# Moving the weight tiles of a float32 decoder kernel to another remainder modulo 256 bytes

## The chip, the cores and the metric

The kernel runs on one NeuronCore of a Trainium2 chip. The metric is the device time of one execution in microseconds. Runs of this kernel lay between 2705.7 and 2709.78 us, with a median of 2706.16 us over three runs.

## What is computed

The reference is a two-layer decoder trunk on a sequence of 1,024 tokens with a width of 1,024, in float32. Layer 0 mixes with a short gated convolution, layer 1 with differential attention (8 heads, two maps of 64 dimensions each) over one shared K and V. Each layer also has a causal convolution FFN (width 2,816, gate and up) and a gated embedding from a per-layer input `p`. Every sub-layer is wrapped in RMSNorm. Cut to what matters here:

```python
def short_conv_mixer(h, w_in, w_conv, w_out):
    gb, gc, u = jnp.split(h @ w_in, 3, axis=-1)
    return (gb * causal_dwconv(gc * u, w_conv)) @ w_out

def conv_ffn(h, w_up, w_conv, w_down):
    gate, up = jnp.split(causal_dwconv(h @ w_up, w_conv), 2, axis=-1)
    return (jax.nn.silu(gate) * up) @ w_down

def per_layer_embed(x, p_i, g_pre, w_gate, w_proj, g_post):
    gate = jax.nn.sigmoid(rms_norm(x, g_pre) @ w_gate)
    return rms_norm(gate * (p_i @ w_proj), g_post)
...
for i in range(DEPTH):
    h = rms_norm(x, g_pre_mix[i])
    mix = short_conv_mixer(...) if i < N_A_LAYERS else diff_attention(...)
    x = x + rms_norm(mix, g_post_mix[i])
    x = x + rms_norm(conv_ffn(rms_norm(x, g_pre_ffn[i]), ...), g_post_ffn[i])
    x = x + per_layer_embed(x, p[i], ...)
```

## The kernel before

**Products.** Activations are held transposed: 128 features on the partitions, 512 tokens (one half of the sequence) along a partition. A float32 product is made from three matmuls on operands of type float32r: each operand is split into a high part (a cast) and a low part (the rest), and high x high, low x high and high x low are added up in PSUM. `mm3` (L323 to L329) does this for one output block of 128 features over 8 input blocks: 24 matmuls. The weight is the stationary operand, a slice of 128 columns of a tile `wh` (high) or `wl` (low); the activation is the moving operand, 512 columns of a pair of tiles, most of them from the pool `hy` (40 tiles) or from an "s" tile of the scope that is open.

**Weights.** `wload` (L175) loads a weight block of 512 KB into a tile `wr`; `wsplit` (L189) or `wcut` (L214) makes `wh` on ScalarE and `wl` on VectorE (L206 to L217). Each of `wr`, `wh`, `wl` has three buffers of 4,096 bytes a partition in the pool `wpool`. A loader works two weight blocks ahead, and the splits one ahead of their use (`emit_all`, L289).

**FFN.** The up projection has three kinds of steps. `std_step` (L781, matmul L796) computes one block for the first half of the tokens, in two parts of 256 columns, 24 matmuls each. `pair_step` (L831) computes a gate block and an up block together by a scheme with seven products instead of eight, each of `product` (L813, matmuls L818 to L820) with 12 matmuls; with `both` set it has 512 columns, without it 256. Its last product uses `A22`, whose split is kept in tiles `w5h` and `w5l` of the scope "up" (L226); the other six use `wh` and `wl` tiles (`pair_split`, L220). The first 8 blocks of layer 0 and the first 7 of layer 1 (`NS`) are done by two `std_step` and later one 256-column `pair_step`, the other 14 and 15 by a 512-column `pair_step`. The down projection (`down_step`, L922, matmuls L935 to L937) reads the hidden activations back from DRAM, splits each into a `c2` tile, and runs 512-column matmuls into four PSUM tiles.

**Attention.** `v_part` (L1136, matmul L1151) has the operands the other way round: the activation `hy` is stationary, and 256 columns of `wh` or `wl` move. `kq_part` uses `mm3` with PSUM tiles `pd`. Scores (L1258), transposes (L1284, L1324) and the product with V (L1299) are interleaved with them. Transposes of the norms are at L367 and L379; those and the others read `ident`, the identity matrix.

**Placement.** Tiles are placed one after another within a partition. Outer pools come first: constants (`cst`, `ident`, `halo`, `gsub`, `neg_lam`), `wpool`, `work` (`acc`, `sq`, small ones, `hn`, `rb`), `hypool`. Behind them lies the scope that is open: "sc" for the convolution layer (tiles `rk`, `c`, `u`, then 24 "s" tiles), "up", "pq" or "att". Tiles that nothing uses (`pad0`, `pad1`, `pad`) take place only. The first constant starts 16,512 bytes into the partition.

```python
nc.tensor.matmul(out, whi[:, c], hi, start=(i == 0), stop=False)
nc.tensor.matmul(out, wlo[:, c], hi, start=False, stop=False)
last_mm[0] = nc.tensor.matmul(out, whi[:, c], lo, start=False, stop=(i == n - 1)).ins
```

Of the kernel before, what the change touches and what calls it, by code (L numbers as in the profile page):

```python
# [9 lines left out]
F32 = mybir.dt.float32  # L10
# [6 lines left out]
S = 1024  # L17
HT = 512
UW = 528
ND = 8  # L20
NF = 22
NH = 8
# [35 lines left out]
def program(tc, a):  # L58
    nc = tc.nc
    ctx = ExitStack()  # L60
    with ctx:
        _program(tc, nc, a, ctx)


def _program(tc, nc, a, ctx):
    P = 128
    ep = ctx.enter_context
    cpool = ep(tc.tile_pool(name="cpool", bufs=1))
    wpool = ep(tc.tile_pool(name="wpool", bufs=3))
    work = ep(tc.tile_pool(name="work", bufs=2))  # L70
# [7 lines left out]
    def nm(s):  # L78
        uid[0] += 1
        return f"{s}_{uid[0]}"  # L80
# [17 lines left out]
    def wk(tag, shape=(P, HT), dt=F32, bufs=2):  # L98
        return work.tile(list(shape), dt, tag=tag, name=nm(tag), bufs=bufs)
# [24 lines left out]
    def own(al, t):  # L124
        owner[id(t)] = (al, t)
        return t
# [20 lines left out]
    cst = cpool.tile([P, C_ALL], F32, tag="cst", name="cst")  # L147
    nc.sync.dma_start(out=cst, in_=a["cvec"])

    cpool.tile([P, 8], F32, tag="pad0", name="pad0")  # L150
    work.tile([P, 8], F32, tag="pad", name="pad", bufs=1)
    ident = cpool.tile([P, P], F32, tag="ident", name="ident")
    make_identity(nc, ident)
    cpool.tile([P, 8], F32, tag="pad1", name="pad1")
    halo = cpool.tile([P, 52, 2], F32, tag="halo", name="halo")
    gsub = cpool.tile([P, 1], F32, tag="gsub", name="gsub")
    nc.vector.tensor_scalar(gsub, cst[:, C_SUB:C_SUB + 1], 1.0 - LAM0, None, ALU.mult)
# [6 lines left out]
    oscr = dpool.tile([2, NH, 2, P, HT], F32, tag="oscr", name="oscr")  # L164
    xscr = dpool.tile([2, ND, P, HT], F32, tag="xscr", name="xscr")
    pscr = dpool.tile([2, ND, P, HT], F32, tag="pscr", name="pscr")
    grep = dpool.tile([NH, P, GLEN], F32, tag="grep", name="grep")
# [101 lines left out]
    cur = []  # L269
# [3 lines left out]
    def free_h(key):  # L273
        slots_of[key].free(2 * ND)

# [134 lines left out]
    def make_h(xs, rb, gname, key, alloc, drop=False):  # L410
        hs = []
        al = alloc if isinstance(alloc, Slots) else alloc()
        for k in range(ND):
            while not al.room(2):
# [17 lines left out]
    def prologue():  # L432

        first = [s_ for s_ in steps if s_["w"] is not None][:2]
        for k in range(ND):
            if k in (PR0, PR1):
# [5 lines left out]
    def gen_first(half):  # L442
        xs = first_x if half == 0 else []
        acc = wk("acc", bufs=3)
        for k in range(len(xs), ND):
            x = own(hy, hy())
# [210 lines left out]
        ys.append(y)  # L657

    def su():
        return cur[0].tile([P, UW], F32, tag="u", name=nm("u"), bufs=3)[:, 0:HT + 2]  # L660

    def sc_():
        if "up" in scopes:
# [3 lines left out]
    def u2():  # L667
        return scopes["up"][1].tile([P, 2, UW], F32, tag="u2", name=nm("u2"), bufs=2)[:, :, 0:HT + 2]

# [40 lines left out]
    def sc_mix(half):  # L710
# [15 lines left out]
        def u_step(f):  # L726
            def fn(w):
                p_ = ps()
                mm3(p_, w[0], w[1], have["mix0", half], k128)
                v = su()  # L730
                nc.vector.tensor_tensor(v[:, 2:], hold["gc"], p_, ALU.mult)
                c = conv(None, v, f, half, C_SC + 3 * f, v[:, 2:])
                if half == 0:
                    nc.vector.tensor_tensor(c, c, have["r", ("mix0", 0)][0], ALU.mult)
                hold["c"] = c
            return fn
# [786 lines left out]
```

## Time and profile before

| what | value |
|---|---|
| median of three runs | 2706.16 us |
| the profiled execution | 2703.73 us |
| its span, from the first to the last instruction | 2701.9 us |
| mean granted TensorE clock | 0.98 |
| TensorE matmul busy | 2581.3 us, 96% |
| TensorE weight load busy | 2137.5 us, 79% |
| VectorE busy | 1866.8 us, 69% |
| ScalarE busy | 1296.4 us, 48% |
| GpSimd busy | 158.1 us, 6% |

A matmul's duration in the profile runs from its start to a modelled end and overlaps with the next one; the time that a row of matmuls takes is read from the starts. Weight loads (PEld) run beside the matmul ahead of them. "hy,wh" in a row means that the instruction reads a moving tile of `hy` and a weight tile `wh`; buffer numbers are left out.

### The profile page before, as it was taken

Reading aid. Unit: us, or ns where it says so; the run is one execution under the profiler, and the core shown is the slowest. Engines: PE = TensorE matmul, PEld = TensorE weight load, DVE = VectorE, ACT = ScalarE, POOL = GpSimd, SP = SyncE. Lnnn points to the kernel's source line nnn. Section 1 sums busy time; section 2 is a strip of 40 time slices with the busy share of each in tenths; the row PEclk is TensorE's granted clock in tenths of the full one; section 3 lists DMA queues with packets and bytes.
Section 4 is the critical chain, followed back from the end, with each engine's and each line's share of the span. In section 5 each row is a group of like instructions: output and inputs, shape, how many; then the busy total and the mean of one; then the engine's idle time right before and its main releaser. Section 6 shows DMA issues by size and latency. Waiting matters only on the chain.

```text
span 2701.9 us, 36095 instructions
## 1 busy us (share of the span) xinstructions
PE 2581.3 (96%) x13438; PEld 2137.5 (79%) x13438; DVE 1866.8 (69%) x3201; ACT 1296.4 (48%) x2216; POOL 158.1 (6%) x328
## 2 busy tenths in 40 slices
PE   8999999899998999997999999899899999899995
PEld 7878889688887878786887878788788888787874
DVE  7546459877797466688666665558977779547667
ACT  5233245444455445556555545446544445445542
POOL 0000003000011000000000000100200001000001
PEclk9999999899999999998999999899999999999998
DMA  5225224222236554333111111266222223656342
GB/s 177 99 91 195 94 90 130 86 86 78 83 109 215 187 205 153 122 121 117 47 48 63 56 48 56 97 217 218 95 86 72 86 78 117 232 188 217 109 171 78
DMA packets 125407, 325.30 MB, mean 120 GB/s; under 512 B 14008, under 2 KB 16352, under 8 KB 125232
## 3 DMA queue, kind: packets, MB, share of 16 engines
q1 hardware_dynamic: 125232, 323.01, 35.0%
q8 instruction: 105, 1.72, 0.3%
q14 instruction: 70, 0.57, 0.1%
HBM read 271.54 MB, written 56.14 MB: 121 GB/s over the span
## 4 chain that ended last, share of the span: by engine, by line
PE 85%; DVE 9%; ACT 2%; DMA 2%; issue 2%; DVEq 0%; SPq 0%; ACTq 0%
PE ps L327 8%; PE ps L328 8%; PE ps L329 8%; PE ps L819 7%; PE ps L820 7%; PE ps L818 7%; PE ps L937 6%; PE ps L936 6%; PE ps L935 6%; PE ps L796 4%; PE pd L1151 4%; PE qk L1258 3%; PE st L1299 2%; PE pd L327 2%; PE pd L328 2%; PE pd L329 2%
## 5 line engine op out<-in xcount | busy, mean ns | idle before, releaser
L211 DVE TENSOR_TENSOR wl<-wr,wh 128x1024 fp32r<-128x1024 f32 x238 | 290.9, 1223 | 231.5 <-ACT wh L210 179.4
L210 ACT CAST wh<-wr 128x1024 fp32r<-128x1024 f32 x238 | 249.9, 1051 | 349.9 <-PE ps L937 148.4
L819 PE MATMUL ps<-hy,wl 128*128 128x512 f32 (+1 forms) x924 | 329.8, 359 | 16.8 <-DVE wl L217 16.8
L818 PE MATMUL ps<-hy,wh 128*128 128x512 f32 (+1 forms) x924 | 316.5, 359 | 13.6 <-ACT wh L216 13.6
L935 PE MATMUL ps<-c,wh 128*128 128x512 f32 x704 | 279.6, 397 | 8.8 <-ACT c L314 8.8
L936 PE MATMUL ps<-c,wl 128*128 128x512 f32 x704 | 279.9, 398 | 0.0
L216 ACT CAST wh<-wr 128x1024 fp32r<-128x1024 f32 x132 | 137.8, 1047 | 209.5 <-PE ps L820 154.2
L937 PE MATMUL ps<-c,wh 128*128 128x512 f32 x704 | 231.2, 397 | 2.0 <-DVE c L315 2.0
L327 PE MATMUL ps<-hy,wh 128*128 128x512 f32 x552 | 218.3, 397 | 8.3 <-ACT hy L399 8.3
L820 PE MATMUL ps<-hy,wh 128*128 128x512 f32 (+1 forms) x616 | 219.2, 357 | 0.0
L328 PE MATMUL ps<-hy,wl 128*128 128x512 f32 x552 | 218.4, 396 | 0.0
L329 PE MATMUL ps<-hy,wh 128*128 128x512 f32 x552 | 217.8, 396 | 0.0
L819 PEld LDWEIGHTS ps<-hy,wl 128*128 128x128 f32 x924 | 174.8, 189 | 48.8 <-DVE wl L217 20.9
L818 PEld LDWEIGHTS ps<-hy,wh 128*128 128x128 f32 x924 | 171.8, 190 | 44.4 <-ACT wh L216 16.6
L217 DVE TENSOR_TENSOR wl<-wr,wh 128x1024 fp32r<-128x1024 f32 x132 | 160.8, 1221 | 17.1 <-ACT wh L216 16.9
L935 PEld LDWEIGHTS ps<-c,wh 128*128 128x128 f32 x704 | 132.8, 189 | 41.1 <-ACT c L314 9.3
L937 PEld LDWEIGHTS ps<-c,wh 128*128 128x128 f32 x704 | 132.7, 189 | 35.9 <-DVE c L315 3.8
L936 PEld LDWEIGHTS ps<-c,wl 128*128 128x128 f32 x704 | 132.8, 189 | 32.5
L314 ACT CAST c<-s 128x512 fp32r<-128x512 f32 x175 | 108.1, 619 | 104.4 <-PE ps L937 93.6
L340 DVE TENSOR_TENSOR acc<-acc,sq 128x512 f32<-128x512 f32 x165 | 112.8, 687 | 61.3 <-ACT sq L339 58.9
L820 PE MATMUL ps<-s,wh 128*128 128x512 f32 (+1 forms) x440 | 154.6, 356 | 0.0
L315 DVE TENSOR_TENSOR c<-s,c 128x512 fp32r<-128x512 f32 x175 | 120.2, 688 | 47.8 <-ACT c L314 47.8
(237 smaller groups left out, 5894.8 us busy)
## 6 DMA issues: line engine op xcount, KB each, us to landing
wr<-w_ffn_up SPq DMA_DIRECT2D x118, 512.0 KB, 3.5
wr<-w_ffn_down SPq DMA_DIRECT2D x88, 512.0 KB, 3.5
s<-hscr SPq DMA_DIRECT2D x175, 256.0 KB, 3.5
wr<-w_sc_in SPq DMA_DIRECT2D x48, 512.0 KB, 3.5
hscr<-c SPq DMA_DIRECT2D x88, 256.0 KB, 2.5
wr<-w_ple_gate SPq DMA_DIRECT2D x32, 512.0 KB, 3.5
xscr<-hy SPq DMA_DIRECT2D x40, 256.0 KB, 4.5
hy<-xscr SPq DMA_DIRECT2D x40, 256.0 KB, 5.6
```

Of the source, the lines that this page charges most:

```text
L210: nc.scalar.copy(out=hi[:, :n], in_=raw[:, :n])
L211: nc.vector.tensor_tensor(lo[:, :n], raw[:, :n], hi[:, :n].bitcast(F32), ALU.subtract)
L217: nc.vector.tensor_tensor(lo, src, hi.bitcast(F32), ALU.subtract)
L327: nc.tensor.matmul(out, whi[:, c], hi, start=(i == 0), stop=False)
L328: nc.tensor.matmul(out, wlo[:, c], hi, start=False, stop=False)
L329: last_mm[0] = nc.tensor.matmul(out, whi[:, c], lo, start=False, stop=(i == n - 1)).ins
L818: nc.tensor.matmul(o, hi[:, c], bh, skip_group_check=True, start=start and j == 0, stop=False)
L819: nc.tensor.matmul(o, lo[:, c], bh, skip_group_check=True, start=False, stop=False)
L820: last_mm[0] = nc.tensor.matmul(o, hi[:, c], bl, skip_group_check=True, start=False, stop=stop and j == 3).ins
L935: nc.tensor.matmul(o, hi[:, c], j[:, 0, :], start=(k == 0), stop=False)
L936: nc.tensor.matmul(o, lo[:, c], j[:, 0, :], start=False, stop=False)
L937: last_mm[0] = nc.tensor.matmul(o, hi[:, c], j[:, 1, :], start=False, stop=(k == NF - 1)).ins
```

## The change

Two unused tiles of 32 bytes among the constants are removed, the unused tile in the work pool grows from 32 to 96 bytes, and the tile `u` of the first layer from 2,112 to 2,304 bytes, of which the same part is used. Nothing else differs.

```diff
+US = 576
...
-    cpool.tile([P, 8], F32, tag="pad0", name="pad0")
-    work.tile([P, 8], F32, tag="pad", name="pad", bufs=1)
+    work.tile([P, 24], F32, tag="pad", name="pad", bufs=1)
     ident = cpool.tile([P, P], F32, tag="ident", name="ident")
     make_identity(nc, ident)
-    cpool.tile([P, 8], F32, tag="pad1", name="pad1")
     halo = cpool.tile([P, 52, 2], F32, tag="halo", name="halo")
...
     def su():
-        return cur[0].tile([P, UW], F32, tag="u", name=nm("u"), bufs=3)[:, 0:HT + 2]
+        return cur[0].tile([P, US], F32, tag="u", name=nm("u"), bufs=3)[:, 0:HT + 2]
```

## Rows read from the trace of the kernel before

**Rows 1.** The page: the span, and TensorE's busy time with its share.

```profile
span 2701.9 us, 36095 instructions
...
PE 2581.3 (96%) x13438; PEld 2137.5 (79%) x13438; DVE 1866.8 (69%) x3201; ACT 1296.4 (48%) x2216; POOL 158.1 (6%) x328
```

**Rows 2.** The page: the chain that ended last, shares of the span by engine.

```profile
PE 85%; DVE 9%; ACT 2%; DMA 2%; issue 2%; DVEq 0%; SPq 0%; ACTq 0%
```

**Rows 3.** Busy time by stage: us, each engine's busy us, granted clock, DMA share, GB/s.

```profile
20.00:368.00 348.00, 348.00 (x1506) 277.87 (x1505) 191.03 (x285) 117.58 (x163) 6.00 (x24) 1.00 0.35 116
...
400.00:450.00 50.00, 50.00 (x440) 50.00 (x439) 44.55 (x77) 27.63 (x44) 13.36 (x18) 1.00 0.53 171
477.00:769.00 292.00, 281.87 (x1242) 229.02 (x1243) 226.76 (x254) 133.26 (x170) 22.98 (x59) 0.98 0.24 83
769.00:870.00 101.00, 89.89 (x657) 82.83 (x657) 87.89 (x129) 56.51 (x91) 14.86 (x15) 0.98 0.54 185
870.00:1086.00 216.00, 214.99 (x929) 172.23 (x928) 130.69 (x187) 103.50 (x154) 0.00 (x0) 1.00 0.53 180
1216.00:1745.00 529.00, 504.81 (x3125) 413.05 (x3123) 338.32 (x967) 283.64 (x719) 31.43 (x75) 0.97 0.19 65
```

**Rows 4.** Groups of matmuls by shape: 512 columns, weight wh (busy us, mean ns).

```profile
L935 PE MATMUL ps<-c,wh 128*128 128x512 f32 x704 | 279.6, 397 | 8.8 <-ACT c L314 8.8
...
L818 PE MATMUL ps<-hy,wh 128*128 128x512 f32 x610 | 235.7, 400 | 13.6 <-ACT wh L216 13.6
...
L327 PE MATMUL ps<-hy,wh 128*128 128x512 f32 x552 | 218.3, 397 | 8.3 <-ACT hy L399 8.3
...
L327 PE MATMUL pd<-hy,wh 128*128 128x512 f32 x288 | 117.6, 408 | 6.8 <-ACT hy L1159 6.5 <-ACT acc L336 0.2
```

**Rows 5.** The same view: weights w5h and w5l, 512 and 256 columns.

```profile
L819 PE MATMUL ps<-hy,w5l 128*128 128x512 f32 x102 | 39.9, 391 | 0.0
L818 PE MATMUL ps<-hy,w5h 128*128 128x512 f32 x102 | 39.7, 389 | 0.0
...
L818 PE MATMUL ps<-hy,w5h 128*128 128x256 f32 x52 | 15.4, 297 | 2.1 <-DVE u L859 2.1
...
L819 PE MATMUL ps<-hy,w5l 128*128 128x256 f32 x52 | 15.0, 288 | 0.0
```

**Rows 6.** The same view: 256 columns with wh, and L1151, where wh moves.

```profile
L796 PE MATMUL ps<-hy,wh 128*128 128x256 f32 x610 | 125.9, 278 | 4.1 <-ACT hy L314 2.8 <-ACT wh L210 1.3
...
L1151 PE MATMUL pd<-wh,hy 128*128 128x256 f32 x512 | 102.0, 292 | 1.4 <-DVE hn L1124 1.4
...
L818 PE MATMUL ps<-hy,wh 128*128 128x256 f32 x314 | 81.2, 281 | 0.0
...
L327 PE MATMUL ps<-s,wh 128*128 128x256 f32 x48 | 13.2, 278 | 0.0
```

**Rows 7.** Timeline of PE, a 512-column pair step: start us, us, instruction.

```profile
700.16 0.39 PE L818 MATMUL ps<-s,w5h 128*128 128x512 f32 x1
...
701.32 0.39 PE L820 MATMUL ps<-s,w5h 128*128 128x512 f32 x1
...
702.91 0.40 PE L819 MATMUL ps<-hy,wl 128*128 128x512 f32 x1
...
705.48 0.39 PE L818 MATMUL ps<-hy,wh 128*128 128x512 f32 x1
```

**Rows 8.** Timeline of PE, a 256-column pair step, matmuls with w5h and w5l.

```profile
780.83 0.28 PE L818 MATMUL ps<-hy,w5h 128*128 128x256 f32 x1
...
781.79 0.28 PE L820 MATMUL ps<-hy,w5h 128*128 128x256 f32 x1
```

**Rows 9.** Timeline of PE, a std_step, matmuls with wh and wl.

```profile
410.10 0.28 PE L796 MATMUL ps<-hy,wl 128*128 128x256 f32 x1
...
412.93 0.28 PE L796 MATMUL ps<-s,wh 128*128 128x256 f32 x1
```

## The prediction, made before the changed kernel was run

> **What bounds the kernel now.** I read the page first, then the stages, then the groups of matmuls by shape, then single starts. The page has TensorE (PE) busy for 96% of the span [rows 1], and the chain that ended last runs through PE for 85% of it and through VectorE (DVE) for 9% [rows 2]. The stages say where that holds. In the first convolution layer (20 to 368 us) and in the down projection (870 to 1086 us) PE has work all the time and DVE is at 55 to 61%; the up projection with 512 columns (477 to 769 us) has PE busy for 97%; attention (1216 to 1745 us) for 95%. One stage is different: the up projection with 256 columns (769 to 870 us) has PE at 90 of 101 us and DVE at 88 [rows 3]. So nearly everywhere the time from one matmul's start to the next one's is the kernel's time, and the question is whether the place of an operand in SBUF sets it.
>
> **Where the tiles lie.** Tiles follow each other in a partition, each size rounded up to 32 bytes. Counting up the sizes, before the change wr, wh and wl start 224 bytes past a multiple of 256; hy, c2 and most "s" tiles start at 160; the "s" tiles of the first layer (scope sc) at 96, since each of three u tiles takes 2,112 bytes; w5h and w5l, the copies for A22, at 160. A slice of 128 or 512 columns keeps these remainders.
>
> **The change, part by part.** (a) Two unused 32-byte tiles go from the constants, so wr, wh and wl move down by 64 bytes, to 160. (b) The unused tile in the work pool grows by 64 bytes, so all that comes after it stays. (c) u in scope sc grows to 2,304 bytes, and the "s" tiles behind it move to 160. (d) ident moves from 224 to 192, halo from 0 to 192. No instruction, transfer or wait is added, removed or moved past another, and no queue changes.
>
> The kernel of before already holds a trial of (a): products with w5h and w5l have the weight at 160 and the moving operand at 160, among neighbours whose weight is at 224. By shape, a 512-column matmul with wh takes 397 to 400 ns [rows 4] and one with w5h or w5l 389 to 391 [rows 5]. With 256 columns it is the other way: 288 to 297 ns with w5 [rows 5] and 278 to 281 with wh [rows 6]. These durations have modelled ends, so I take starts instead. From 702.91 to 705.48 us there are 11 steps with wh and wl: 2.57 / 11 = 233.6 ns. From 700.16 to 702.91 there are 12 with w5: 229.2 ns; the first five are still uneven and the last seven, from 701.32, take 1.59 / 7 = 227.1 ns [rows 7]. With 256 columns, eight steps with w5 take 781.79 - 780.83 = 0.96 us, 120.0 ns each [rows 8], and 25 with wh and wl 412.93 - 410.10 = 2.83 us, 113.2 ns each [rows 9]. So the weight's place is worth about -6.6 ns with 512 columns and +6.8 ns with 256: a trade, and the counts decide.
>
> Counts follow from the code (three matmuls a product):
> - 512 columns outside attention: 2,712 in mm3 (64 output blocks of the first layer, 29 of the gates and 12 of the last output projection at 24 each, and 32 of the small projections at 6), 2,088 in product without w5 (29 steps x 72), 2,112 in down_step. Sum 6,912 x -6.6 ns = **-45.6 us**. The mean with the uneven start (229.2) would give 4.4 ns, -30.4 us; I take the settled value, since w5 runs are only 12 long and here a run goes on. 384 of these have their moving "s" tile at 96 today; part (c) brings them to the same pair 160 and 160, and is counted here.
> - 512 columns within attention: 864 (pd) [rows 4]. They alternate with other matmuls and keep leaving the settled rhythm: between 0 and -5.7 us, I take the middle, **-2.9 us**. Waits for DVE there, if PE comes earlier, eat the rest.
> - 256 columns in std_step: 15 x 2 x 48 = 1,440. From 400 to 450 us PE has no gap [rows 3], so +6.8 ns each is paid in full: **+9.8 us**. A further 144 at the very end of the kernel (mm3, 278 ns [rows 6]): **+1.0 us**.
> - 256 columns in pair_step: 15 steps x 72 = 1,080, at most +7.3 us. PE idles 11 of 101 us there [rows 3], so a longer product first fills the idle time left by DVE and the loads of wr; that cover gone, it would be paid. I take **+1 us**, and keep 0 and 7.3.
> - v_part: here hy is the weight, at 160 already, and wh is the moving operand: 768 matmuls at 292 ns [rows 6], next to w5's 288 to 297. So 0 to +1.7 us if its mixed rhythm settles at 120 ns; **+1 us**.
> - ident, halo, u: transposes have their data at other places, and none of them shows with two places of ident. Their 544 matmuls could move by what the 256-column ones do, 6.8 ns either way: between -3.7 and +3.7 us, taken as **0**. The cast into wh and the difference into wl (L210 to L217) write at the new place. PE's work covers them in every stage but the up projection with 256 columns, so elsewhere they cost nothing as long as PE is the later one; in that stage, if DVE's 88 us moved by the 3% by which the matmuls do, it would be 2.6 us either way. No row shows one shape of them at both places, and I take **0**.
>
> Sum: -45.6 - 2.9 + 9.8 + 1.0 + 1 + 1 = -35.7 us. The profiled execution took 2703.73 us (its span 2701.9), so 2668.0; the median of the runs is 2.4 us above it, so about **2670 us**, 1.3% faster.
>
> The Trainium skill speaks against any gain: "TensorE: Matmul & The Clock Gate", section "Back-to-back issue gap", gives a warm step as columns over 2.4 GHz plus 2.5 ns, an estimate of 215.8 ns for 512 columns and 109.2 for 256, with no term for the place of an operand. By that rule the change is worth 0. The trace disagrees: it shows 227 and 234 ns for one shape within 6 us [rows 7], and 113 and 120 for the other [rows 8, 9].
>
> **The rivals.**
> 1. *The place makes no difference*; the shorter step belongs to w5 for another reason (far up in SBUF, last product of a step). For it: w5 differs from wh in more than the remainder. Against: hy, s and c2 lie far apart and step alike with wh, and v_part, whose weight hy is in the middle of SBUF at 160, shows the 256-column duration of w5. A placement other than I counted belongs here too. Time 2706. The Trainium skill's rule above would give this time as well.
> 2. *The other side: only the loss lands.* The 512-column matmuls fall into the uneven rhythm of the first five w5 matmuls (231 to 236 ns) and do not settle, while each 256-column one pays 6.8 ns: +9.8 + 1.0 + 7.3 + 1.7 = +20, **2726**. It decides when the gain per 512-column matmul is below (9.8 + 1.0) / 6,912 = 1.6 ns. Against: the run in [rows 7] settles within six.
> 3. *Half a gain.* Groups of 24 matmuls settle late each time, or DVE becomes the limit of the up stage with 512 columns (227 of 292 us busy today [rows 3]): 4.4 ns instead of 6.6, and the 256-column pair_step in full: -30.4 + 9.8 + 1.0 + 7.3 + 1.7 = -10.6, **2695**.
>
> **How the numbers follow.** Forecast 0.74, rival 1 0.08, rival 2 0.06, rival 3 0.12. A measurement of this kernel can tell about 0.2%, 5.4 us, from no change. The forecast and rival 3 are faster by more than that: 0.86. Rival 1 is the same: 0.08. Rival 2 is slower: 0.06. The forecast's own bounds: at best every 512-column matmul gains 6.7, attention in full, and nothing is paid with 256 columns in pair_step: -46.3 - 5.7 + 10.8 - 3.7 = -45, and if the 256-column ones keep 113 ns as well, -56; at worst 5.5 ns, attention 0, every loss in full: -38.0 + 9.8 + 1.0 + 7.3 + 1.7 + 3.7 = -14.5. That is 2650 to 2692. Leaving out the far corner at the low end, I give 2655 to 2692.
>
> **What would show it.** Down projection: 228 ns or less from start to start, and the stage shorter by 2.8%, some 6 us of 216. std_step: 120 ns, 50 us becomes 53. The 256-column up stage: nearly the same length with less idle time on PE. First layer: both weight and moving operand at 160, so 227 ns with w_sc_out too. The prediction is wrong if wh products keep 233 ns, or if the 256-column ones do not move, or if a saving in PE's stages comes back as a wait for DVE.

## The result, and the profile after

The changed kernel takes 2666.98 us (median of four runs, 2663.2 to 2670.5) against 2705.93 us for the kernel of before on the same chip: a ratio of 0.9854, 95% interval 0.9842 to 0.9867. The profiled execution took 2663.2 us, 40.5 us less than the profiled one of before (it is the fastest of the four runs; the medians differ by 39.0).

The page of the changed kernel, span, TensorE's busy time and the chain that ended last, shows the same picture as [rows 1, 2]: 38 of the 40.5 us have left PE's busy time, and PE is still busy for 96%. The kernel has not changed its bound; its bound has become shorter.

```profile
span 2661.4 us, 36095 instructions
...
PE 2543.3 (96%) x13438; PEld 2151.7 (81%) x13438; DVE 1866.8 (70%) x3201; ACT 1297.4 (49%) x2216; POOL 156.1 (6%) x328
...
PE 84%; DVE 9%; ACT 2%; issue 2%; DMA 2%; POOL 0%; DVEq 0%; SPq 0%; ACTq 0%; POOLq 0%
```

Line numbers of the changed kernel are one lower here (L818 is L817). The stages of [rows 3], in its columns, cut in the changed kernel at the same matmuls (both kernels run their matmuls in the same order but for ten of 13,438, and the counts agree with [rows 3] line by line); the second line is the `std_step` stretch:

```profile
19.29:358.17 338.88, 338.88 (x1506) 278.41 (x1505) 191.35 (x286) 118.14 (x164) 6.00 (x24) 1.00 0.35 119
392.43:444.76 52.33, 52.33 (x440) 52.33 (x439) 44.80 (x76) 27.73 (x44) 12.14 (x18) 1.00 0.48 160
471.44:756.02 284.58, 274.46 (x1242) 228.43 (x1243) 227.07 (x254) 134.60 (x173) 28.43 (x59) 0.98 0.25 86
756.02:858.15 102.13, 91.84 (x657) 86.08 (x657) 87.85 (x128) 56.68 (x91) 14.63 (x15) 0.97 0.54 182
858.15:1068.54 210.39, 209.11 (x929) 172.52 (x928) 130.56 (x187) 103.65 (x154) 0.00 (x0) 1.00 0.55 185
1195.22:1721.43 526.21, 499.74 (x3125) 412.24 (x3123) 339.12 (x969) 283.62 (x719) 31.44 (x75) 0.97 0.19 66
```

For the same matmuls the convolution layer is shorter by 9.1 us (348.0 to 338.9), the 512-column up stage by 7.4 (292.0 to 284.6), the down projection by 5.6 (216.0 to 210.4), attention by 2.8 (529.0 to 526.2). The 256-column up stage is longer by 1.1 (101.0 to 102.1). The granted clock (the third column from the right) stands within 0.01 of before in every stage, so the clock has no part in it. The second line is the loser: the 440 matmuls that took 50.0 us before take 52.3, because `std_step`'s 256-column matmuls step more slowly.

The groups of matmuls by shape (busy us, mean ns, idle time in front) say the same of single shapes. Those that answer to [rows 4 to 6]: with 512 columns the mean falls by 3 to 7 ns, and only for the `wh` and `wl` groups; w5h stays at 389. With 256 columns and `wh` it rises from 278 to 286, and in `v_part` (L1150) from 292 to 295. Two rows with `wl` are added for an experiment below.

```profile
L934 PE MATMUL ps<-c,wh 128*128 128x512 f32 x704 | 277.0, 394 | 8.8 <-ACT c L313 8.8
...
L818 PE MATMUL ps<-hy,wl 128*128 128x512 f32 x610 | 239.4, 392 | 7.9 <-DVE wl L216 7.9
L817 PE MATMUL ps<-hy,wh 128*128 128x512 f32 x610 | 231.7, 393 | 10.9 <-ACT wh L215 10.9
...
L326 PE MATMUL ps<-hy,wh 128*128 128x512 f32 x552 | 215.4, 392 | 8.1 <-ACT hy L398 8.1
...
L795 PE MATMUL ps<-hy,wh 128*128 128x256 f32 x610 | 132.4, 286 | 3.7 <-ACT hy L313 2.4 <-ACT wh L209 1.3
...
L326 PE MATMUL pd<-hy,wh 128*128 128x512 f32 x288 | 116.6, 405 | 6.6 <-ACT hy L1158 6.4 <-ACT acc L335 0.3
...
L1150 PE MATMUL pd<-wh,hy 128*128 128x256 f32 x512 | 103.2, 295 | 1.4 <-DVE hn L1123 1.4
...
L818 PE MATMUL ps<-hy,wl 128*128 128x256 f32 x314 | 88.4, 287 | 7.8 <-DVE wl L216 7.8
...
L817 PE MATMUL ps<-hy,w5h 128*128 128x512 f32 x102 | 39.7, 389 | 0.0
```

As the ends are modelled, the starts decide. The timeline of PE (start us, us, instruction) in a `std_step` and in a 512-column pair step, first and last row of each stretch:

```profile
409.29 0.28 PE L795 MATMUL ps<-hy,wl 128*128 128x256 f32 x1
...
411.69 0.28 PE L795 MATMUL ps<-s,wh 128*128 128x256 f32 x1
...
690.98 0.39 PE L818 MATMUL ps<-hy,wl 128*128 128x512 f32 x1
...
693.47 0.62 PE L817 MATMUL ps<-hy,wh 128*128 128x512 f32 x2
```

With 256 columns there are 20 steps in 2.40 us, 120.0 ns (113.2 in [rows 9]); with 512 there are 11 in 2.49 us, 226.4 ns (233.6 in [rows 7]). Both are the values that w5h and w5l had in the kernel of before.

### The profile page after: what moved, and what is told of

Its sections match the earlier page's. It is cut to its first block, busy times and chain, and to the rows that moved or that the text cites. A ratio compares the mean times of both kernels' runs of the same rounds, so it can differ in the third digit from the quotient of the medians.

```text
span 2661.4 us, 36095 instructions
## 1 busy us (share of the span) xinstructions
PE 2543.3 (96%) x13438; PEld 2151.7 (81%) x13438; DVE 1866.8 (70%) x3201; ACT 1297.4 (49%) x2216; POOL 156.1 (6%) x328
## 4 chain that ended last, share of the span: by engine, by line
PE 84%; DVE 9%; ACT 2%; issue 2%; DMA 2%; POOL 0%; DVEq 0%; SPq 0%; ACTq 0%; POOLq 0%
PE ps L326 7%; PE ps L328 7%; PE ps L327 7%; PE ps L818 7%; PE ps L819 7%; PE ps L817 7%; PE ps L936 6%; PE ps L934 6%; PE ps L935 6%; PE ps L795 5%; PE pd L1150 4%; PE qk L1257 3%; PE pd L326 2%; PE pd L327 2%; PE pd L328 2%; PE st L1298 2%
## 5 line engine op out<-in xcount | busy, mean ns | idle before, releaser
L818 PE MATMUL ps<-hy,wl 128*128 128x512 f32 (+1 forms) x924 | 327.8, 357 | 15.7 <-DVE wl L216 15.7
L817 PE MATMUL ps<-hy,wh 128*128 128x512 f32 (+1 forms) x924 | 313.4, 356 | 10.9 <-ACT wh L215 10.9
L934 PE MATMUL ps<-c,wh 128*128 128x512 f32 x704 | 277.0, 394 | 8.8 <-ACT c L313 8.8
L936 PE MATMUL ps<-c,wh 128*128 128x512 f32 x704 | 227.8, 393 | 2.6 <-DVE c L314 2.6
L326 PE MATMUL ps<-hy,wh 128*128 128x512 f32 x552 | 215.4, 392 | 8.1 <-ACT hy L398 8.1
L328 PE MATMUL ps<-hy,wh 128*128 128x512 f32 x552 | 215.0, 391 | 0.0
L818 PEld LDWEIGHTS ps<-hy,wl 128*128 128x128 f32 x924 | 175.6, 190 | 43.9 <-DVE wl L216 19.8
L817 PEld LDWEIGHTS ps<-hy,wh 128*128 128x128 f32 x924 | 172.7, 190 | 36.1 <-ACT wh L215 11.9
```

The costliest lines, as they stand in the source:

```text
L817: nc.tensor.matmul(o, hi[:, c], bh, skip_group_check=True, start=start and j == 0, stop=False)
L818: nc.tensor.matmul(o, lo[:, c], bh, skip_group_check=True, start=False, stop=False)
L934: nc.tensor.matmul(o, hi[:, c], j[:, 0, :], start=(k == 0), stop=False)
L936: last_mm[0] = nc.tensor.matmul(o, hi[:, c], j[:, 1, :], start=False, stop=(k == NF - 1)).ins
```

## The experiments

Two kernels hold matmuls alone and measure the step itself; the others are the whole kernel with one thing changed. The diffs of the whole kernels are against the kernel of before. The matmuls-only kernels leave the decoder out altogether, so their times are only times of matmuls. A "step" is the time from one matmul's start to the next one's.

**1. map: is it the weight's place, or both places together?** Eight pairs of weight tiles (high, low) and eight pairs of moving tiles start at remainders 0, 32, ... 224 modulo 256. Every weight pair is run with every moving pair, 48 matmuls in the kernel's pattern of three, first with 512 columns and then with 256.

```python
for n in (512, 256):
    for w in STEPS:
        for m in STEPS:
            for k in range(16):
                ...
                nc.tensor.matmul(o, W[w][0][:, s], M[m][0][:, 0:n], start=(k == 0), stop=False)
                nc.tensor.matmul(o, W[w][1][:, s], M[m][0][:, 0:n], start=False, stop=False)
                nc.tensor.matmul(o, W[w][0][:, s], M[m][1][:, 0:n], start=False, stop=(k == 15))
```

> The kernel's matmul pattern alone (high x high, low x high, high x low, float32r), 48 matmuls for each pair of a weight remainder and a moving remainder modulo 256 (0, 32, .. 224 for each), first with 512, then with 256 columns; the rest of the computation is left out. Theory (the remainders of the pair set the step): weight 160 with moving 160 steps 227 ns with 512 columns and 120 ns with 256; weight 224 with moving 160 steps 233 and 113; the two ends of the table differ by several ns. Rival A (only the weight's remainder counts): each weight has one value along all moving remainders, 227 for 160 and 233 for 224, within 1 ns. Rival B (only the difference of the two remainders counts): all eight equal pairs step 227 and 120, and all pairs that are 64 apart 233 and 113. Rival C (the place in low bits makes nothing): all 64 pairs within 1 ns of each other at either width.

The timeline of PE in this kernel, in time order: the first and the last start of a settled stretch of 35 steps, for five pairs with 512 columns and then two with 256. Remainders are counted from the tile sizes and the place of the first constant; the difference of two tiles needs the sizes alone. The second letter of a tile is its remainder: b is 32, f is 160, h is 224 (so `wf` is a weight at 160 and `mh` a moving tile at 224; `n` is the low part of a moving tile).

```profile
466.94 0.39 PE L47 MATMUL ps<-mb,wf 128*128 128x512 f32 x1
...
475.08 0.39 PE L49 MATMUL ps<-nb,wf 128*128 128x512 f32 x1
...
511.70 0.39 PE L47 MATMUL ps<-mf,wf 128*128 128x512 f32 x1
...
519.63 0.39 PE L49 MATMUL ps<-nf,wf 128*128 128x512 f32 x1
...
533.82 0.39 PE L47 MATMUL ps<-mh,wf 128*128 128x512 f32 x1
...
541.83 0.39 PE L49 MATMUL ps<-nh,wf 128*128 128x512 f32 x1
...
689.83 0.40 PE L47 MATMUL ps<-mf,wh 128*128 128x512 f32 x1
...
698.00 0.39 PE L49 MATMUL ps<-nf,wh 128*128 128x512 f32 x1
...
712.14 0.39 PE L47 MATMUL ps<-mh,wh 128*128 128x512 f32 x1
...
720.08 0.40 PE L49 MATMUL ps<-nh,wh 128*128 128x512 f32 x1
...
977.61 0.28 PE L47 MATMUL ps<-mf,wf 128*128 128x256 f32 x1
...
981.81 0.28 PE L49 MATMUL ps<-nf,wf 128*128 128x256 f32 x1
...
1068.50 0.28 PE L47 MATMUL ps<-mf,wh 128*128 128x256 f32 x1
...
1072.47 0.28 PE L49 MATMUL ps<-nf,wh 128*128 128x256 f32 x1
```

Divided by 35: weight 160 with moving 32 takes 232.6 ns, 160 with 160 226.6, 160 with 224 228.9, 224 with 160 (the kernel of before) 233.4, and 224 with 224 226.9. So a weight at 160 is fast only with a moving tile at 160, and a weight at 224 is as fast with a moving tile at 224. Over all 64 pairs with 512 columns the step depends on the difference of the two remainders alone: 226.7 where they are equal, 228.8 where the moving tile lies 64 past the weight, 232.4 to 234.3 everywhere else. With 256 columns 160 with 160 takes 120.0 and 224 with 160 takes 113.4; equal remainders give 120.0 at all eight places. But the 113 ns does not come for every pair at that difference: of the pairs whose moving tile lies 64 before the weight, two show 113.3 and the other six 117.8. Of the expectation's readings, rival B held for the equal pairs; that pairs 64 apart are alike did not hold, since 64 past the weight (228.8 and 117.8) is not 64 before it (233.4).

**2. a_only: the weights' move without the longer `u`.** The first layer's 384 output matmuls then have the weight at 160 and the moving tile at 96.

```diff
-    cpool.tile([P, 8], F32, tag="pad0", name="pad0")
-    work.tile([P, 8], F32, tag="pad", name="pad", bufs=1)
+    work.tile([P, 24], F32, tag="pad", name="pad", bufs=1)
...
-    cpool.tile([P, 8], F32, tag="pad1", name="pad1")
```

> The change without its part (c): weights at 160, the moving tiles of the first layer's output projection back at 96 (384 matmuls of 512 columns). Theory: the time stays within 2 us of the changed kernel, 2665 to 2669 us at its median, since 384 matmuls at 160 over 96 can lose at most the 5.6 ns that they gained, 2.2 us; their step shows whether the moving tile's place counts: 227 ns if it does not, more if it does. Rival A (only the weight's place): exactly 227 ns there. Rival B (only the difference): about 233 ns or another value than 227 there. If part (c) is what carries the gain, this kernel goes back towards 2706.

Measured 2669.36 us (2667.53 to 2673.73), ratio 0.9877 (0.9862 to 0.9891). That is just above the expected 2665 to 2669. Those 384 matmuls step at 233.3 ns, and at 226.8 with the whole change (means over the stretches' starts): 384 x 6.5 ns = 2.5 us. The times alone can't show so little: this kernel is 34.1 us faster than the kernel of before on its chip (2703.43), the changed kernel 39.0 than on its own (2705.93), and the intervals of the two ratios overlap. Part (a) is nearly the whole gain.

**3. c_only: the longer `u` without the weights' move.** The same 384 have 224 and 160 instead of 224 and 96.

```diff
-        return cur[0].tile([P, UW], F32, tag="u", name=nm("u"), bufs=3)[:, 0:HT + 2]
+        return cur[0].tile([P, 576], F32, tag="u", name=nm("u"), bufs=3)[:, 0:HT + 2]
```

> Part (c) alone: weights stay at 224, the moving tiles of the first layer's output projection go from 96 to 160. Theory: these 384 matmuls go from 232.4 to 233.3 ns, +0.3 us, so no change that can be measured, 2704 to 2708 us. Rival: if the moving tiles' place alone carries the gain, the time falls here by some us and a_only loses them.

Measured 2704.33 us, ratio 1.0003 (0.9994 to 1.0013): nothing that can be measured, and their step goes from 232.4 to 233.3 ns, as expected. Part (c) is worth its 2.5 us only together with (a): it is not the place of a moving tile that pays, but its agreement with the weight.

**4. equal224: everything at 224, nothing at 160.** The weights stay where the kernel of before has them; the moving tiles come to them, by the longer unused tile in the work pool and the longer `u`.

```diff
-    work.tile([P, 8], F32, tag="pad", name="pad", bufs=1)
+    work.tile([P, 24], F32, tag="pad", name="pad", bufs=1)
...
-        return cur[0].tile([P, UW], F32, tag="u", name=nm("u"), bufs=3)[:, 0:HT + 2]
+        return cur[0].tile([P, 576], F32, tag="u", name=nm("u"), bufs=3)[:, 0:HT + 2]
```

> The kernel before with everything behind the weights moved up by 64 bytes (pad in the work pool 96 bytes, u 2,304 bytes): weights stay at 224, and all moving operands of the dense products come to 224. No operand of a dense product starts at 160. Theory of the prediction (160 is the good place for a weight): time as before, 2700 to 2707 us, with steps of 233 and 113 ns. Theory after the table of remainders (the two operands must start at the same remainder, whichever it is): as the changed kernel, 2663 to 2671 us, with 227 ns for 512 columns and 120 ns for 256.

Measured 2665.88 us (2664.37 to 2668.19), ratio 0.986 (0.9843 to 0.9876): the gain of the change, without the change to the weights. The down projection's group of matmuls by shape in this kernel, which has the 277 us of the changed one and not the 279.6 of [rows 4]:

```profile
L935 PE MATMUL ps<-c,wh 128*128 128x512 f32 x704 | 276.5, 393 | 8.8 <-ACT c L314 8.8
```

And its timeline of PE in a 512-column pair step:

```profile
690.69 0.39 PE L819 MATMUL ps<-hy,wl 128*128 128x512 f32 x1
...
693.41 0.39 PE L818 MATMUL ps<-hy,wh 128*128 128x512 f32 x1
```

Twelve steps in 2.72 us are 226.7 ns, and `std_step` has its 120 ns (119.9). This settles which of the two readings holds: "weights at 160" is not what counts, "weight and moving operand at the same remainder" is.

**5. map2: how fine is it, how long does it remember, and does the type matter?** One pair of weight tiles at remainder 0, and moving slices that start at 0 to 496 bytes into one tile. Then single stretches with one of the two weight tiles, or both, moved by 64 bytes, after different predecessors; then the same with bf16 operands.

```python
for n in (512, 256):
    for o in OFFS:
        sweep(n, o)
for n in (512, 256):
    lone(n, 16, 16, 0, 24)
    lone(n, 0, 0, 0, 8)
    lone(n, 16, 0, 0, 24)
    lone(n, 0, 0, 0, 8)
    lone(n, 0, 16, 0, 24)
for r in range(4):
    lone(512, 0, 0, 0, 3 + r)
    lone(256, 16, 16, 0, 24)
for n in (512, 256):
    for o in (0, 16, 32, 48, 64, 96, 112):
        half(n, o)
```

> Matmuls alone again, the rest is left out. First the moving operand's distance from the weight's remainder in finer steps: 4, 8, 12 bytes, then 0 to 496 in steps of 16, 48 matmuls each, at 512 and at 256 columns. Theory (only the difference modulo 256 counts): distances of 256 and more repeat those below; 0 gives 226.7 and 64 gives 228.8 ns at 512 columns; what lies between the multiples of 32 is open. Rival (it is a matter of whole lines of some size): steps of 16 bytes form plateaus that are the same for all distances within a line, and 4 to 12 bytes off is as good as 0. Then 256 columns with the weight 64 bytes past the moving operand after different predecessors: if the step there depends on what ran before, some of these settle at 113 ns and others at 118; with one of the two weights (high or low part) moved alone, the step lies at 113 too if the pair of operands in one matmul decides, and elsewhere if the change from one matmul to the next does. Last bfloat16 operands at seven distances: no effect expected at 512 columns if the cost comes from 4-byte weights, the same pattern if from the streams as such.

The settled steps, worked out from the starts (bytes from the weight's remainder to the moving operand's, then ns with 512 and with 256 columns):

```
  0: 226.7 120.0     4: 236.6 123.4     8: 233.3 116.7    12: 228.9 116.7
 16: 231.6 118.7    32: 233.3 116.7    48: 233.3 118.3    64: 228.8 117.8
 80: 231.1 119.9    96: 233.2 120.0   112: 231.3 113.3   128: 232.4 118.7
144: 233.3 118.7   160: 234.3 117.3   176: 233.3 119.4   192: 233.4 113.3
208: 234.7 119.3   224: 233.4 118.4   240: 226.7 117.1   256: 226.6 120.0
```

From 256 to 496 bytes every value repeats the one 256 lower, within 0.1 ns. With 512 columns there is one more fast place, 16 bytes before the weight (240: 226.7). With 256 columns the equal place, 120.0, is among the slowest, and 113.3 stands at 112 and 192. With a weight 64 past the moving tile (192 in the table) and 256 columns, the stretch settled at 113.4 ns after one predecessor and at 117.8 after four others: the same operands have two rhythms. Which predecessor leads to which was not found: in map seven stretches with these distances followed one at distance 160, and two of them settled at 113.3, five at 117.8. With only the high or only the low weight moved it was 117.8 (256 columns) and 231.2 (512). With the low weight alone, two of three matmuls have equal places, and the mean of their own steps would be (2 x 226.7 + 233.4) / 3 = 228.9: the step is not a mean over single matmuls.

With bf16 the place did nothing. The timeline of PE, 96 matmuls of 512 columns apart, across two such places (a row covers 12 matmuls):

```profile
739.77 2.75 PE L59 MATMUL ps<-mb,wb 128*128 128x512 bf16 x12
...
760.49 2.75 PE L59 MATMUL ps<-mb,wb 128*128 128x512 bf16 x12
```

20.72 us / 96 = 215.8 ns (two of the 96 have no record; each shows as a gap of two steps), and the stretches at all seven places lie within 0.1 of it; with 256 columns all give 109.1 or 109.2. The bf16 places were multiples of 32 bytes; 4 to 12 bytes were not tried. The formula of the Trainium skill, "TensorE: Matmul & The Clock Gate", section "Back-to-back issue gap", given there for an isolated matmul and weighed in the prediction, comes to an estimate of 215.8 and 109.2 ns: these bf16 runs agree with it, and the float32r runs do not, neither in the size (226.7 to 236.6) nor in having no place in it.

**6. apart64: does the table foretell a whole kernel?** Weights at 160, moving tiles at 224: the second-best difference.

```diff
-    cpool.tile([P, 8], F32, tag="pad0", name="pad0")
-    work.tile([P, 8], F32, tag="pad", name="pad", bufs=1)
+    work.tile([P, 40], F32, tag="pad", name="pad", bufs=1)
...
-    cpool.tile([P, 8], F32, tag="pad1", name="pad1")
...
-        return cur[0].tile([P, UW], F32, tag="u", name=nm("u"), bufs=3)[:, 0:HT + 2]
+        return cur[0].tile([P, US], F32, tag="u", name=nm("u"), bufs=3)[:, 0:HT + 2]
```

> The changed kernel with everything behind the weights moved up by 64 bytes more: weights at 160, moving operands at 224, w5h and w5l at 224 too. The table gives 228.8 ns for a moving operand 64 bytes past the weight with 512 columns and 117.8 with 256. If the table of remainders foretells whole kernels, against before: 6,912 x -4.5 = -31 us, attention about -2, std_step 1,440 x +3.7 = +5.3, the end +0.6, so about -27: 2676 to 2681 us, between the two kernels. Rival (equal remainders are all that helps, every other pair is as before): 2700 to 2707. Rival (any pair but the old one is good): 2663 to 2671.

Measured 2676.31 us (2674.82 to 2677.79), ratio 0.9895 (0.9878 to 0.9912), at the low end of what the table gave. The timeline of PE in a 512-column pair step:

```profile
689.74 0.39 PE L817 MATMUL ps<-s,wh 128*128 128x512 f32 x1
...
692.49 0.39 PE L817 MATMUL ps<-s,w5h 128*128 128x512 f32 x1
```

Twelve steps in 2.75 us are 229.2 ns, where the table has 228.8; `std_step` has 117.2 as the mean of its steps without waits, where the table has 117.8: most of its stretches settle at 117.8 and seven of 60 at 113.3.

**7. two_places, one_place, two_places_b: a better version.** The 256-column matmuls of `std_step` lose 6.8 ns by the change. In two_places each of the three buffers of `wh` and `wl` is a tile of its own, five of the six with 64 bytes to spare, and there the steps marked late (`std_step` and the last gates) write and read their weight 64 bytes further on, at 224, while all others stay at 160. The small tiles are set between them so that the remainders come out. one_place is the same kernel without the 64 bytes; two_places_b is two_places a second time, beside one_place.

```diff
+    def weight(tag, n, late=False):
+        i = turn[tag] % 3
+        turn[tag] += 1
+        size = 1024 if (tag, i) == ("wl", 2) else 1040
+        q = 16 if late and size > 1024 else 0
+        return cpool.tile([P, size], F32R, tag=f"{tag}{i}", name=nm(tag), bufs=1)[:, q:q + n]
...
-        hi = wpool.tile([P, 1024], F32R, tag="wh", name=nm("wh"))
-        lo = wpool.tile([P, 1024], F32R, tag="wl", name=nm("wl"))
+        hi, lo = (weight(t, 1024, st_.get("late")) for t in ("wh", "wl"))
```

and in one_place:

```diff
-        q = 16 if late and size > 1024 else 0
+        q = 0
```

> A version that takes both ends of the trade: wh and wl get 64 bytes of slack and start at 224 for std_step and the last gate steps (256 columns, moving operand at 160) and at 160 for all else; the third wl buffer has no slack and stays at 160. The small tiles fill the gaps between the weight tiles. If the 256-column step falls back to the 113 to 114 ns that it had before, std_step gains about 1,440 x 5.9 x 2/3 plus a third of that for the steps with the third wl buffer (117.8 ns), 6 to 8 us against the changed kernel: 2657 to 2661 us. Rival (that rhythm depends on what ran before, and settles at 118 here): 2 ns for each, 3 us, 2662 to 2666. Rival (the slack and the new order of tiles cost a wait): as the changed kernel or slower.

> The layout of two_places (own tags for the three buffers of wh and wl, small tiles in the gaps) with no offset: all weights start at 160, 256-column steps too. In two_places the std_step matmuls settled at 118 instead of 120 ns (-5.4 us against the changed kernel), and the 5.5 and 3.7 us in which PE waits for a wl split early in each 512-column pair phase were gone. If the place gives the first and the own tags the second, this kernel has 120 ns in std_step and no such waits: 2657 to 2662 us, between two_places and the changed kernel. Rival (the offset is behind both): 2663 to 2670, as the changed kernel. Rival (the place gives nothing): as two_places, 2652 to 2656.

> two_places once more beside one_place on the same chip, so that the two can be compared: 2652 to 2657 us. one_place is slower by 4 to 6 us if the 256-column place counts, and the same within 2 us if not.

two_places: 2653.87 us (2652.57 to 2654.94), ratio 0.9812 (0.9797 to 0.9827). It gained more than was forecast (2657 to 2661 us), but not by the 113 ns that the forecast was built on. The timeline of PE in a `std_step` of two_places:

```profile
408.25 0.28 PE L827 MATMUL ps<-hy,wl 128*128 128x256 f32 x1
...
410.48 0.28 PE L827 MATMUL ps<-s,wh 128*128 128x256 f32 x1
```

19 steps in 2.23 us are 117.4 ns: the slower of the two rhythms, not the 113.2 of [rows 9]. Both rhythms are in both kernels. Cut into 60 groups of 24 matmuls, the steps of `std_step` settle at 113.3 in most groups of the kernel of before and at 117.8 in six; in two_places it is 117.8 in most and 113.3 in six. In two_places a third of the blocks also have their low weight still at 160.

one_place, with `std_step` at 120 ns, took 2658.95 us (2657.47 to 2664.33), ratio 0.9837 (0.9824 to 0.9851), and two_places_b, beside it on the same chip, 2657.0 (2655.61 to 2660.64), ratio 0.9825 (0.9811 to 0.9838). By the expectation's own fork (4 to 6 us if the 256-column place counts, within 2 if not) the 64 bytes are not shown to gain time: the 2 us lie within the intervals. What the traces do show is the shorter step, 117.4 against 120.0 ns; the sums over the starts of `std_step`, 178.4 us in one_place, 174.8 and 176.7 in the two runs of the other, differ hardly more than those of two kernels with the same steps (178.4 in equal224, 180.2 in the changed kernel). Most of the gain over the changed kernel comes with the tiles' own places in the layout: one_place is 46.4 us faster than the kernel of before on its chip, the changed kernel 39.0, and their profiled spans differ by 5.2 us. Here too the intervals of the ratios overlap, so the size of this gain is uncertain.

What the layout alone brought is easily misread. The waits of PE in one_place show `wl` (L248) at 2.8 us, where the changed kernel has 15.7 (shown below), and that looks like the whole answer. Groups of matmuls by shape in one_place, beside the four of L817 and L818 above, show where the wait went:

```profile
L850 PE MATMUL ps<-hy,wl 128*128 128x512 f32 x610 | 238.8, 392 | 0.0
L849 PE MATMUL ps<-hy,wh 128*128 128x512 f32 x610 | 236.8, 395 | 12.0 <-ACT wh L247 12.0
...
L850 PE MATMUL ps<-hy,wl 128*128 128x256 f32 x314 | 89.2, 289 | 3.0 <-DVE wl L248 2.8
L849 PE MATMUL ps<-hy,wh 128*128 128x256 f32 x314 | 85.5, 289 | 10.8 <-ACT wh L247 10.8
```

With 512 columns the 7.9 us of waiting for `wl` are gone and `wh` rises by 1.1 only; with 256 columns the wait moved from `wl` (7.8 to 3.0) to `wh` (0 to 10.8). By sums over the starts, the 512-column pair steps are 7.1 us shorter than in the changed kernel, the 256-column ones 3.1 us longer, the down projection 3.0 us shorter, the large products of mm3 2.6 us longer, and all together 5.3 us shorter; the spans differ by 5.2 (2661.4 and 2656.2). Only the first of these is clearly more than such sums differ by between kernels with the same steps. Whether the tile of its own for each buffer or the new order of the small tiles moves these waits, and why, was not tried.

## Why the prediction was right, and where its reason was not

The forecast was 2670 us (-35.7 for the profiled execution); measured were 2667 and -40.5. The time from start to start, summed over each kind of matmul in the traces of the two kernels, lets each term be held against its own measurement:

```
                                    predicted  before   after  difference
512 columns, mm3                                648.8   629.5   -19.3
512 columns, pair, wh and wl                    515.2   498.0   -17.2
512 columns, down projection                    502.4   491.3   -11.1
  together                             -45.6                    -47.6
512 columns, attention (pd)             -2.9    216.3   213.0    -3.3
256 columns, std_step                   +9.8    170.1   180.2   +10.1
256 columns, end                        +1.0     29.6    30.5    +0.9
256 columns, pair, wh and wl                    141.5   143.9    +2.4
256 columns, pair, w5h and w5l          -        34.4    31.9    -2.5
  together                              +1                       -0.1
v_part                                  +1      108.6   109.5    +0.9
transposes and others, 128 columns       0      150.7   151.0    +0.3
512 columns, pair, w5h and w5l           -       79.5    78.9    -0.6
scores, 256 to 512 columns               -       86.0    85.2    -0.9
sum                                    -35.7                    -40.3
```

A dash marks work for which the prediction has no term of its own. Such sums hold PE's idle time too, which differs between traces of kernels with the same steps: equal224 has 633.0 for mm3 and 178.4 for `std_step`, the changed kernel 629.5 and 180.2. Differences of some 3 us in one line are not to be read.

- **512 columns outside attention, -45.6.** Right: 6.6 ns was taken from seven steps of w5, and 6.7 ns is what map measures between 224 with 160 and equal places. The choice of the settled value was right as well. A run of 512-column matmuls with new places settles within about six steps, as in [rows 7], and here the runs go on. The down projection gave 2.8 us less than 2,112 x 6.6 ns = 13.9, though its step went from 233.3 to 226.9 ns as well: PE idles a little more there. The pair steps gave 3.4 us more than 2,088 x 6.6 ns = 13.8: part of PE's waits went too, since those for `wh` in these steps fell by 2.7 us, from 13.6 [rows 4] to 10.9. The waits of PE in the changed kernel, us in total, times, longest us:

```profile
PE ps L818 <- DVE wl L216: 15.7, 15, 4.9
...
PE ps L817 <- ACT wh L215: 10.9, 2, 5.7
```

- **Attention, -2.9.** Right (-3.3), a middle between two bounds that could as well have missed. `std_step`, **+9.8**, and the end, **+1.0**: right, and paid in full as PE has no gap there.
- **256-column pair steps, +1.** Right, by two effects that cancel, of which one was foreseen. The longer steps are there: without waits, those with `wh` and `wl` go from 113.9 to 119.9 ns, which alone would be +6.5 us for 1,080. Their sum rises by 2.4 only, so some 4 us went into PE's idle time, the cover that was forecast. The sum of w5's own steps fell by 2.5 us, which was not foreseen and makes this line's zero. Their settled step stayed (119.5 and 119.8 ns); what went are steps of over 135 ns, 34 of the 180 before and 10 after. Before, w5's stretches followed matmuls at another difference of remainders, and now they don't, which fits; no run took that apart. The stage itself went from 101.0 to 102.1 us in layer 0.
- **v_part, +1; transposes and casts, 0.** Right as far as such sums tell.
- **The rivals.** Rival 1 (the place makes no difference) falls with the measured time, and with map, where nothing but the place differs. Rival 2 (512 columns never settle) falls with the 226.4 ns in the pair step. Rival 3 (half a gain, DVE as the limit) falls with the -47.6 us of the 512-column matmuls and with the up stage, where DVE is busy for 227 of 285 us and PE's waits for the pair split did not grow.

**The step that failed** is the sentence "the weight's place is worth about -6.6 ns with 512 columns and +6.8 ns with 256". The trial that the kernel of before holds had only one moving remainder, 160, in it, so it could not tell "weight at 160" from "weight where the moving operand is". equal224 and map tell: the weight's place alone is worth nothing. The prediction did count the 384 matmuls at 96 as gaining only through part (c), which is the right rule, but gave no reason; a_only and c_only show it. The forecast came out all the same because in this change both readings foretell one time: the moving tiles of nearly all dense products lie at 160, so a weight at 160 is also a weight at their place. That is luck of the layout. The second half of the sentence failed in another way: 113 ns with 256 columns is not the price of a place. It is one of two rhythms, and two_places, which put most of its weights back at 224 for these matmuls, got the other one, 117.4.

What stays open: why equal remainders make float32r matmuls step faster, and with 256 columns slower. The runs show the pattern and its period; none shows the cause.

## What to carry to other kernels

When a kernel is bound by float32r matmuls of 512 columns from start to start, count up where the weight tile and the moving tile begin modulo 256 and make the two equal: here it was worth 6.7 of 233.4 ns in each matmul and 1.5% of the whole, by taking out two unused tiles and lengthening two others. Look first for a product in the kernel's own trace that already has another difference, compare starts rather than modelled durations, and ask what in that product differs besides the thing you mean to change. A placement for 512 columns is not one for 256, and a price read from a short stretch may be a rhythm that depends on what ran before.

## What the chip showed that was not expected

- The step of float32r matmuls with 512 columns goes by the difference of the two operands' remainders modulo 256, whatever the remainders are: 226.7 ns at 0 and at 240, 228.8 at 64, 228.9 at 12, 231 to 237 elsewhere. bf16 matmuls of the same shape take 215.8 ns at every place measured.
- Four bytes are enough: with 512 columns a moving operand 4 bytes past the weight's remainder steps at 236.6 ns, the slowest of all, and 8 bytes at 233.3 (one stretch of 48 matmuls each).
- With 256 columns the order is another (113.3 to 123.4 ns, equal places 120.0), and the same operands settled at 113.4 or at 117.8 ns depending on the matmuls that came before.
- One of the two weights at the equal place is not enough: with only the high or only the low one moved off it by 64 bytes the 512-column step was 231.2 ns, between 226.7 and 233.4, and in both cases the same.
